# A fp32 encoder block as weight products by Strassen's scheme: activation forms, weight parts and product sums put in another order on VectorE and ScalarE

## The chip, the core and the metric

One core of a Trainium2 chip runs the whole block in one launch. The metric is device microseconds of one execution. In the profile PE is TensorE, PEld its weight loads, DVE is VectorE, ACT is ScalarE, POOL is GpSimd, and SP queues most of the loads.

## The reference

512 tokens of 2048 features pass one encoder block in float32; the feed-forward width is 5632.

```python
h = rms_norm(x, norm_mix); z = h @ w_in                      # q, k, v, u, gates a and b
y_a = chunked_rel_attention(q, k, v, rel_bias)               # 16 heads of 64
y_b = multiscale_pool(u, pool_w, pool_scale)
merged = sigmoid(z_ga) * (y_a @ w_branch_a) + sigmoid(z_gb) * (y_b @ w_branch_b)
x = x + merged @ w_out                                       # 2048 x 2048
gu = rms_norm(x, norm_ffn) @ w_gate_up                       # 2048 x 2*5632
x = x + (silu(gu[:, :5632]) * gu[:, 5632:]) @ w_down         # 5632 x 2048
return rms_norm(x, norm_final)
```

## The kernel before

Each float32 operand is used as two parts, a high one rounded to TensorE's fp32r type and a low one, the rest: ScalarE copies the high part out (`hi`, `hiw`), VectorE subtracts (`lo`, `low`). A product of two such operands is three matmuls.

The first 988 us make the projections of `w_in`, the attention, the pooling and the two branch products, panel by panel. The last gate panels and branch-a panels stand apart (`N_TAIL`): first the gates, then the branch products, whose results make `merged`.

From there on the kernel runs **jobs**. A job multiplies 512 tokens by a block of 1024 weight rows and 2 x 512 weight columns, split two by two in tokens, rows and columns, and needs seven block products instead of eight (`PRODUCTS`: P1, P5, P6, P3, P7, P2, P4, in this order). The left factor of a product is a **form**: a sum or difference of activation blocks (P1 is a11, P5 a22-a21, P6 minus that plus a11, P7 a11-a21, P3, P2, P4 in the same way), split in high and low. The right factor is a weight block or a running sum of blocks: the adds L842 to L848 (`t_to`) work in place on the raw blocks r11, r12, r22, r21. A product has two halves, so a job has 14 **steps** of twelve matmuls each (four for the row pairs and token halves, three for the parts). At step i the code

- queues the raw loads of step i+7 (`load2_to`), the add of step i+3 (`t_to`) and the high part of step i+2 (`hi2_to`, L856);
- issues the twelve matmuls (L893 to L895) into a PSUM bank pair;
- at a product's end takes the bank out: copies of P1, P5, P6 and, without accumulation, of P4 on ScalarE (L899, L904, L909, L929), sums of P3, P7, P2 and else P4 on VectorE (L911, L916, L922, L926);
- calls `step()`, which lets every waiting piece of other work (a generator) issue one portion;
- queues the low part of step i+2 (`lo2_to`, L864).

There are three buffers each for the high and the low parts, two bank pairs of kind x (P1, P6, P7 and P4 of one job share one), one of kind y (P5 with P3, then P2), and two single banks a for transposes. The jobs come in the order of a list: 4 with `w_out` (o), 11 with the first 1024 rows of `w_gate_up` (g 0), then 11 with its other rows (g 1) and among them those with `w_down` (d), two for each block of 1024 hidden rows. 5632 hidden rows are five and a half blocks; the half block (one half a product, seven steps a job) comes last.

The other work: after each o job of the second row block the new x is squared for the norm, transposed on TensorE (L953), scaled (L962) and made into forms for `w_gate_up` (`x1_ready`); after each g 1 job silu and gate times up (`hidden`, L1017, L1020), transposes, and forms for `w_down` (`build_down`). `build_forms` makes a form a step for one half of a form set: the copy L737 of a portion is on ScalarE, the sums L729 to L732 and the subtractions L740, L742 on VectorE; a subtraction waits for the copy of the same form. In the last two jobs POOL multiplies by the weight of the last norm (L1079), and after the last product the row norms and eight output tiles each on ScalarE (L1101) and VectorE (L1098) follow.

Of the kernel before, what the change touches and what calls it, by code (L numbers as in the profile page):

```python
# [40 lines left out]
N_TAIL = 3  # L41
# [5 lines left out]
def hybrid_block_kernel(  # L47
# [672 lines left out]
    def build_forms(forms, h, half):  # L720
# [8 lines left out]
        plan = [("P1", a11, 1, None), ("P5", s, 1, lambda: tt(s, a22, a21, op=ALU.subtract)),  # L729
                ("P6", s, -1, lambda: tt(s, s, a11, op=ALU.add)),  # L730
                ("P3", s, 1, lambda: tt(s, s, a12, op=ALU.subtract)),
                ("P7", s3, 1, lambda: tt(s3, a11, a21, op=ALU.subtract)), ("P2", a12, 1, None), ("P4", a22, 1, None)]  # L732
        for p, src, sign, make in plan:
            if make:
                make()
            hi, lo = forms[p][:, prs, 0], forms[p][:, prs, 1]
            nc.scalar.activation(hi, src, AF.Copy, scale=float(sign))  # L737
            yield
            if sign > 0:
                tt(lo, src, hi.bitcast(F32), op=ALU.subtract)  # L740
            else:
                nc.vector.scalar_tensor_tensor(lo, src, -1.0, hi.bitcast(F32), op0=ALU.mult, op1=ALU.subtract)  # L742
# [125 lines left out]

    def run_job(j):
        forms = j.forms  # L870
        X = Y = Z = None
        a = p5 = u2 = None
        for n, p in enumerate(PRODUCTS):
            if p == "P1":
                X = ps = bank2("x")
            elif p == "P5":
                Y = ps = bank2("y")
            elif p == "P2":
                Z = ps = bank2("y")
            else:  # L880
                ps = Y if p == "P3" else X
            for h in range(j.nh):
# [3 lines left out]
                hi2_to(i + SPLIT)  # L886
                hi, lo = wide(hi_t.pop(-1 - i)), wide(lo_t.pop(-1 - i))
                for t in range(2):
                    for k in range(2):
# [5 lines left out]
                        mm(ps[:, t], fl, hi[:, k], start=False, stop=last, skip_group_check=True)  # L895
                if h == j.nh - 1:
                    if p == "P1":
                        a = ctile()
                        nc.scalar.activation(a, X, AF.Copy)  # L899
                        if j.acc:  # L900
                            nc.gpsimd.dma_start(a, j.acc["11"], accum_op=ALU.add)
                    elif p == "P5":
                        p5 = ctile()
                        nc.scalar.activation(p5, Y, AF.Copy, scale=-1.0)  # L904
                        if j.acc:
                            nc.gpsimd.dma_start(p5, j.acc["22"], accum_op=ALU.add)
# [283 lines left out]
    while active or later:  # L1190
        step()
# [23 lines left out]
```

## Time and profile before

| | |
|---|---|
| median of 3 runs | 2541.85 us (2539.72 to 2542.73) |
| the profiled execution | 2541.46 us, of which the span of its instructions is 2539.5 us |
| busy share of the span, PE / PEld / DVE / ACT / POOL | 97% / 79% / 68% / 46% / 6% |
| mean granted clock of TensorE | 0.992 |
| HBM | 289.44 MB read, 60.86 MB written |

Matmuls overlap, so a busy PE says little of how much it could still gain; the starts of consecutive matmuls say more.

### The profile page before, as it was taken

The page shows a single profiled execution, that of the slowest core. Times are in us where ns is not written, and L with a number is a line of the kernel's source. Part 1 is how long each engine was busy: PE and PEld are TensorE (multiplying, and loading weights), DVE is VectorE, ACT ScalarE, POOL GpSimd, SP SyncE. Part 2 cuts the span into 40 slices and gives each one's busy share as a digit, 9 for nine tenths or more (in the row PEclk, how much of TensorE's full clock was granted, in tenths as well). Part 3 has the DMA queues.
Part 4 walks back from the last instruction along what each step waited for, and adds up shares of the span by engine and source line. Part 5 has one row for each costly group of instructions (what it writes and reads, how often), then busy time and mean ns, then how long its engine had stood idle before and what let it go on. Part 6 is the DMA issues. An engine that isn't in the chain of part 4 may idle for free.

```text
span 2539.5 us, 29049 instructions
## 1 busy us (share of the span) xinstructions
PE 2455.2 (97%) x11221; PEld 2002.9 (79%) x11221; DVE 1732.6 (68%) x1996; ACT 1163.4 (46%) x1499; POOL 151.3 (6%) x242
## 2 busy tenths in 40 slices
PE   9999999999999998999999999999999999999995
PEld 7888888888888887777788888877878778787773
DVE  6445556533343327978877777888897888879885
ACT  5444443322232224466545445555554555555554
POOL 0000000000000000110000000000000001000014
PEclk9999999999999999999999999999999999999997
DMA  5322222323333336664443543645645646637374
GB/s 175 96 86 78 86 92 85 94 92 100 94 101 115 107 106 199 187 211 136 179 163 141 195 156 146 203 117 167 161 145 144 171 133 165 182 104 203 100 214 118
DMA packets 203146, 352.20 MB, mean 139 GB/s; under 512 B 11304, under 2 KB 95856, under 8 KB 202880
## 3 DMA queue, kind: packets, MB, share of 16 engines
q1 hardware_dynamic: 177760, 263.76, 30.9%
q0 software_dynamic: 24096, 84.49, 14.2%
q8 instruction: 88, 1.44, 0.2%
q10 hardware_dynamic: 1152, 2.10, 0.2%
q14 instruction: 50, 0.41, 0.0%
HBM read 289.44 MB, written 60.86 MB: 138 GB/s over the span
## 4 chain that ended last, share of the span: by engine, by line
PE 86%; DVE 8%; issue 3%; ACT 2%; DMA 1%; ACTq 0%; SPq 0%; POOL 0%; DVEq 0%; POOLq 0%
PE psd L211 10%; PE psd L212 10%; PE psd L213 10%; PE psx L893 8%; PE psx L894 8%; PE psx L895 8%; PE psy L893 7%; PE psy L895 7%; PE psy L894 7%; DVE low L864 3%; PE psd L423 1%; DVE fP L740 1%; PE psd L425 1%; PE psd L424 1%; ACT hiw L856 1%
## 5 line engine op out<-in xcount | busy, mean ns | idle before, releaser
L864 DVE TENSOR_TENSOR low<-r,hiw 128x1024 fp32r<-128x1024 f32 x518 | 630.4, 1225 | 133.7 <-ACT hiw L856 131.4
L856 ACT ACTIVATE hiw<-r 128x1024 fp32r<-128x1024 f32 x518 | 546.5, 1057 | 377.0 <-PE psx L895 157.6
L893 PE MATMUL psx<-low,fP 128*128 128x512 f32 x1184 | 471.7, 398 | 29.7 <-DVE low L864 25.2
L894 PE MATMUL psx<-hiw,fP 128*128 128x512 f32 x1184 | 463.3, 391 | 0.0
L895 PE MATMUL psx<-hiw,fP 128*128 128x512 f32 x1184 | 463.1, 391 | 0.0
L168 DVE TENSOR_TENSOR lo<-raw,hi 128x1024 fp32r<-128x1024 f32 (+1 forms) x161 | 195.9, 1218 | 322.8 <-ACT hi L159 322.6
L893 PE MATMUL psy<-low,fP 128*128 128x512 f32 x888 | 353.1, 398 | 23.9 <-DVE low L864 21.8
L159 ACT ACTIVATE hi<-raw 128x1024 fp32r<-128x1024 f32 (+1 forms) x161 | 169.2, 1053 | 427.5 <-PE psd L213 309.7
L895 PE MATMUL psy<-hiw,fP 128*128 128x512 f32 x888 | 348.3, 392 | 0.0
L894 PE MATMUL psy<-hiw,fP 128*128 128x512 f32 x888 | 348.1, 392 | 0.0
L211 PE MATMUL psd<-xh,lo 128*128 128x512 f32 x864 | 341.5, 395 | 0.0
L213 PE MATMUL psd<-xl,hi 128*128 128x512 f32 x864 | 336.7, 390 | 0.0
L212 PE MATMUL psd<-xh,hi 128*128 128x512 f32 x864 | 336.6, 390 | 0.0
L893 PEld LDWEIGHTS psx<-low,fP 128*128 128x128 f32 x1184 | 222.9, 188 | 103.5 <-DVE low L864 55.4
L895 PEld LDWEIGHTS psx<-hiw,fP 128*128 128x128 f32 x1184 | 223.1, 188 | 48.1
L894 PEld LDWEIGHTS psx<-hiw,fP 128*128 128x128 f32 x1184 | 223.1, 188 | 42.3
L893 PEld LDWEIGHTS psy<-low,fP 128*128 128x128 f32 x888 | 168.1, 189 | 68.4 <-DVE low L864 29.0
L895 PEld LDWEIGHTS psy<-hiw,fP 128*128 128x128 f32 x888 | 168.1, 189 | 36.1
L894 PEld LDWEIGHTS psy<-hiw,fP 128*128 128x128 f32 x888 | 168.5, 190 | 32.9
L211 PEld LDWEIGHTS psd<-xh,lo 128*128 128x128 f32 x864 | 162.2, 188 | 36.3 <-issue 2.4
L213 PEld LDWEIGHTS psd<-xl,hi 128*128 128x128 f32 x864 | 162.2, 188 | 34.3
L212 PEld LDWEIGHTS psd<-xh,hi 128*128 128x128 f32 x864 | 162.4, 188 | 31.9
(207 smaller groups left out, 2810.7 us busy)
## 6 DMA issues: line engine op xcount, KB each, us to landing
r<-in_w_gate_up SPq DMA_DIRECT2D x176, 512.0 KB, 7.6
raw<-in_w_in SPq DMA_DIRECT2D x127, 512.0 KB, 3.6
r<-in_w_down SPq DMA_DIRECT2D x88, 512.0 KB, 6.5
x1d<-c POOLq DMA_DIRECT2D x48, 512.0 KB, 8.0
gp<-c POOLq DMA_DIRECT2D x44, 512.0 KB, 6.0
c<-gp POOLq DMA_DIRECT2D x33, 512.0 KB, 5.2
r<-in_w_out SPq DMA_DIRECT2D x32, 512.0 KB, 9.2
raw<-in_w_branch_b SPq DMA_DIRECT2D x16, 512.0 KB, 3.3
```

The source lines that it names most:

```text
L159: nc.scalar.activation(hi_t[i][:, :m], raw_t[i][:, :m], AF.Copy)
L168: nc.vector.tensor_tensor(lo_t[i][:, :m], raw_t[i][:, :m], hi_t[i].bitcast(F32)[:, :m], op=ALU.subtract)
L211: mm(ps, wl, ah, start=start, stop=False)
L212: mm(ps, wh, ah, start=False, stop=False)
L213: mm(ps, wh, al, start=False, stop=stop)
L423: mm(o, XH[kk][:, tok], hi[:, k], start=first, stop=False, skip_group_check=True)
L424: mm(o, XH[kk][:, tok], lo[:, k], start=False, stop=False, skip_group_check=True)
L856: nc.scalar.activation(hi_t[-1 - i], source(i), AF.Copy)
L864: nc.vector.tensor_tensor(lo_t[-1 - i], source(i), hi_t[-1 - i].bitcast(F32), op=ALU.subtract)
L893: mm(ps[:, t], fh, lo[:, k], start=first, stop=False, skip_group_check=True)
L894: mm(ps[:, t], fh, hi[:, k], start=False, stop=False, skip_group_check=True)
L895: mm(ps[:, t], fl, hi[:, k], start=False, stop=last, skip_group_check=True)
```

## The change

- `build_forms`: the order of the forms is now P1, P5, P7, P6, P2, P3, P4. Each step issues ScalarE's copy of one form and VectorE's subtraction of the form of the step ahead. Both differences that need no other form are made first.
- `run_job`: the low part of step i+2 is queued ahead of the matmuls of step i, and the end of a product (`evacuate`) is put on a list that is run in the `step()` of the following step, so it is queued one step later than before and behind that step's add, high and low part.
- `x1_turned`: the transposes of x1 wait until both token halves of a column block are there, and turn 512 tokens at a time with one ScalarE copy per 128 columns; the squares are a piece of work by themselves.
- Order of the jobs: the half block of hidden rows is now the first of `w_down` (it needs the first g 1 job alone), and the d jobs follow the odd g 1 jobs. The forms of the last block go to form set B, when all g jobs have run.
- `N_TAIL` is 4: four gate panels, then four branch-a panels.
- Last norm: the multiplication by its weight is on VectorE; the last block takes it with its scaling in one operation; nine of the sixteen output tiles go through ScalarE, none of them from the last block. The ends of P2 and P4 of the last job are issued without the delay.

```diff
@@ build_forms
+        plan = [("P1", a11, 1), ("P5", s, 1), ("P7", s3, 1), ("P6", s, -1), ("P2", a12, 1), ("P3", s, 1), ("P4", a22, 1)]
+        def low(p, src, sign):
+            hi, lo = forms[p][:, prs, 0].bitcast(F32), forms[p][:, prs, 1]
+            if sign > 0:
+                tt(lo, src, hi, op=ALU.subtract)
+            else:
+                nc.vector.scalar_tensor_tensor(lo, src, -1.0, hi, op0=ALU.mult, op1=ALU.subtract)
+        tt(s, a22, a21, op=ALU.subtract)
+        tt(s3, a11, a21, op=ALU.subtract)
+        for n, (p, src, sign) in enumerate(plan):
+            nc.scalar.activation(forms[p][:, prs, 0], src, AF.Copy, scale=float(sign))
+            if n:
+                low(*plan[n - 1])
+            if n == 2:
+                tt(s, s, a11, op=ALU.add)
+            elif n == 4:
+                tt(s, s, a12, op=ALU.subtract)
+            yield
+        low(*plan[-1])
@@ evacuate, new
+        if p in ("P1", "P5", "P6"):
+            blk = {"P1": "11", "P5": "22", "P6": "12"}[p]
+            o[blk] = ctile()
+            nc.scalar.activation(o[blk], ps, AF.Copy, scale=1.0 if p == "P1" else -1.0)
+            if j.acc and p != "P6":
+                nc.gpsimd.dma_start(o[blk], j.acc[blk], accum_op=add)
+            return
+        blk = {"P3": "12", "P7": "22", "P2": "11", "P4": "21"}[p]
+        if p != "P4":
+            nc.vector.tensor_tensor(o[blk], o[blk], ps, op=add if p == "P2" else sub)
...
+        j.done(blk, o[blk])
@@ run_job
                 hi2_to(i + SPLIT)
+                lo2_to(i + SPLIT)
                 hi, lo = wide(hi_t.pop(-1 - i)), wide(lo_t.pop(-1 - i))
...
+                step()
                 if h == j.nh - 1:
...
-                        nc.vector.tensor_tensor(u2, u2, Y, op=ALU.subtract)
...
-                step()
-                lo2_to(i + SPLIT)
+                    later.append(lambda p=p, ps=ps: evacuate(j, p, ps, o))
+                    if j is jobs[-1] and p in ("P2", "P4"):
+                        step()
@@ x1
+    def x1_turned(p, fb, cs):
+        half = yield from new_half()
+        for n in range(4):
+            ps = bank2("a")
+            for tt in range(NT):
+                nc.tensor.transpose(ps[:, tt * P:(tt + 1) * P], cs[tt // 2][:, tt % 2, n * P:(n + 1) * P], ident)
+            yield
+            m = KD + p * 8 + fb * 4 + n
+            nc.scalar.activation(half[:, n // 2, n % 2], ps, AF.Copy, scale=gains[:, m:m + 1])
@@ build_down, the order of the jobs
-        b, h = p // 2, p % 2
-        while b < n_down - 1 and down_run[0] < 2 * b:
+        b, h = (p + 1) // 2, (p + 1) % 2 if p else 0
+        last = b == n_down - 1
+        while gates_run[0] < NG if last else down_run[0] < 2 * b:
...
-        if p >= 2 and p % 2 == 0 and p < NG - 1:
-            order += [("d", p // 2 - 1, 0), ("d", p // 2 - 1, 1)]
+        if p % 2 and p < NG - 2:
+            order += [("d", p // 2, 0), ("d", p // 2, 1)]
...
-            npair = min(NPAIR, (KF - 8 * b) // 2)
+            npair = NPAIR if b else NPAIR // 2
@@ last_done
-                nc.gpsimd.tensor_tensor(y[:, t], y[:, t], gf[:, f0:f0 + 512], op=ALU.mult)
-                yield
+                if (p, blk) != FINAL:
+                    nc.vector.tensor_tensor(y[:, t], y[:, t], gf[:, f0:f0 + 512], op=ALU.mult)
+                    yield
```

**A g 1 job in which forms are built.** On VectorE, in the second g 1 job, around the end of P3 (the sum of c and psy, L911 before, L889 now); low232 to low235 are the low parts of P7's and P2's four steps, fP1 to fP7 forms, s their sums. Before:

```order
L864 TENSOR_TENSOR low232_12352<-r12_916_12080,hiw232_12335 128x1024
L911 TENSOR_TENSOR c_933_12319<-c_933_12319,psy_926_12229 128x1024
L740 TENSOR_TENSOR fP5_934_12323<-s_935_12329,fP5_934_12323 128x2x256
L730 TENSOR_TENSOR s_935_12329<-s_935_12329,half_924_12220 128x512
L864 TENSOR_TENSOR low233_12375<-r12_919_12103,hiw233_12356 128x1024
L742 SCALAR_TENSOR_TENSOR fP6_934_12324<-s_935_12329,fP6_934_12324 128x2x256
L731 TENSOR_TENSOR s_935_12329<-s_935_12329,half_924_12220 128x512
L864 TENSOR_TENSOR low234_12396<-r21_928_12253,hiw234_12379 128x1024
```

And of the changed kernel:

```order
L872 TENSOR_TENSOR low233_12341<-r12_918_12084,hiw233_12339 128x1024
L735 TENSOR_TENSOR fP1_934_12325<-half_925_12224,fP1_934_12325 128x2x256
L872 TENSOR_TENSOR low234_12361<-r21_927_12231,hiw234_12359 128x1024
L889 TENSOR_TENSOR c_933_12322<-c_933_12322,psy_923_12203 128x1024
L735 TENSOR_TENSOR fP5_934_12326<-s_935_12332,fP5_934_12326 128x2x256
L746 TENSOR_TENSOR s_935_12332<-s_935_12332,half_925_12224 128x512
L856 TENSOR_TENSOR r21_927_12231<-r21_927_12231,r11_914_12026 128x1024
L872 TENSOR_TENSOR low235_12385<-r21_929_12255,hiw235_12383 128x1024
L735 TENSOR_TENSOR fP7_934_12329<-s3_935_12333,fP7_934_12329 128x2x256
```

The low part of P7's second half (low233) stood behind the sum of P3, a form and a form's sum; now it, and the next one too (low234), stand ahead of that sum.

**The first job.** On VectorE, from the last branch-a panel (L664, L665: the gated result `merged`) into the first `w_out` job; low1 and low2 are the low parts of its steps P1 (second half) and P5 (first half), r11 its running sums. Before:

```order
L665 TENSOR_TENSOR sg_633_7318<-sg_571_5718,sg_633_7318 128x512
L864 TENSOR_TENSOR low1_7576<-r11_643_7498,hiw1_7574 128x1024
L742 SCALAR_TENSOR_TENSOR fP6_634_7330<-s_646_7533,fP6_634_7330 128x2x256
L731 TENSOR_TENSOR s_646_7533<-s_646_7533,half_638_7372 128x512
L740 TENSOR_TENSOR fP3_634_7331<-s_646_7533,fP3_634_7331 128x2x256
L732 TENSOR_TENSOR s3_646_7534<-half_638_7372 128x512
L740 TENSOR_TENSOR fP7_634_7332<-s3_646_7534,fP7_634_7332 128x2x256
L740 TENSOR_TENSOR fP2_634_7333<-half_638_7372,fP2_634_7333 128x2x256
L740 TENSOR_TENSOR fP4_634_7334<-half_638_7372,fP4_634_7334 128x2x256
L842 TENSOR_TENSOR r11_642_7496<-r11_642_7496,r12_647_7605 128x1024
L842 TENSOR_TENSOR r11_643_7498<-r11_643_7498,r12_648_7607 128x1024
L864 TENSOR_TENSOR low2_7642<-r11_642_7496,hiw2_7616 128x1024
```

And of the changed kernel:

```order
L735 TENSOR_TENSOR fP3_632_7261<-s_642_7463,fP3_632_7261 128x2x256
L664 TENSOR_TENSOR sg_631_7248<-psd_646_7518,sg_631_7248 128x512
L665 TENSOR_TENSOR sg_631_7248<-sg_571_5718,sg_631_7248 128x512
L872 TENSOR_TENSOR low1_7586<-r11_644_7511,hiw1_7584 128x1024
L735 TENSOR_TENSOR fP4_632_7264<-half_636_7302,fP4_632_7264 128x2x256
L850 TENSOR_TENSOR r11_643_7509<-r11_643_7509,r12_647_7605 128x1024
L850 TENSOR_TENSOR r11_644_7511<-r11_644_7511,r12_648_7607 128x1024
L872 TENSOR_TENSOR low2_7618<-r11_643_7509,hiw2_7616 128x1024
L852 TENSOR_TENSOR r11_643_7509<-r11_643_7509,r22_649_7609 128x1024
```

Five form subtractions and two form sums stood between low1 and the adds of the job's P5; one subtraction is left there, since a branch-a panel more runs while the forms are made.

**The last job.** On POOL before, the multiplications by the last norm's weight gf behind the accumulating loads:

```order
L906 DMA c_1306_18322<-x1d122_5896 128x1024
L913 DMA c_1307_18341<-x1d112_5894 128x1024
L1079 TENSOR_TENSOR c_1306_18322<-c_1306_18322,gf_18124 128x512 x2
L1079 TENSOR_TENSOR c_1304_18297<-c_1304_18297,gf_18124 128x512
L1079 TENSOR_TENSOR c_1307_18341<-c_1307_18341,gf_18124 128x512
L1079 TENSOR_TENSOR c_1304_18297<-c_1304_18297,gf_18124 128x512
L1079 TENSOR_TENSOR c_1308_18377<-c_1308_18377,gf_18124 128x512
L1079 TENSOR_TENSOR c_1307_18341<-c_1307_18341,gf_18124 128x512
L1079 TENSOR_TENSOR c_1308_18377<-c_1308_18377,gf_18124 128x512
```

On VectorE in the changed kernel, at the last job's P7 and P2 (L889), with low516 and low517 the last weight parts:

```order
L872 TENSOR_TENSOR low516_18333<-r21_1304_18203,hiw516_18331 128x1024
L889 TENSOR_TENSOR c_1306_18239<-c_1306_18239,psx_1301_18142 128x1024
L1085 TENSOR_TENSOR c_1306_18239<-c_1306_18239,gf_17860 128x512
L872 TENSOR_TENSOR low517_18354<-r21_1305_18221,hiw517_18352 128x1024
L1085 TENSOR_TENSOR c_1307_18276<-c_1307_18276,gf_17860 128x512
L1085 TENSOR_TENSOR c_1306_18239<-c_1306_18239,gf_17860 128x512
L889 TENSOR_TENSOR c_1303_18200<-c_1303_18200,psy_1308_18329 128x1024
L1085 TENSOR_TENSOR c_1307_18276<-c_1307_18276,gf_17860 128x512
L1085 TENSOR_TENSOR c_1303_18200<-c_1303_18200,gf_17860 128x512 x2
```

The multiplications now stand between VectorE's sums and weight parts; POOL keeps only its loads.

## Rows read from the trace of the kernel before

**Rows 1.** The page, busy time by engine and the granted clock in 40 slices.
```profile
PE 2455.2 (97%) x11221; PEld 2002.9 (79%) x11221; DVE 1732.6 (68%) x1996; ACT 1163.4 (46%) x1499; POOL 151.3 (6%) x242
...
PEclk9999999999999999999999999999999999999997
```

**Rows 2.** Windows: us, busy us (count) of PE, PEld, DVE, ACT, POOL; clock, DMA, GB/s.
```profile
987.80:1079.81 92.01, 81.97 (x337) 63.91 (x336) 80.57 (x84) 46.37 (x54) 11.75 (x14) 0.96 0.71 205
...
1117.98:1257.18 139.20, 128.63 (x570) 100.78 (x568) 119.59 (x129) 88.25 (x138) 9.10 (x15) 0.99 0.47 161
1333.38:1371.48 38.10, 38.10 (x170) 31.32 (x168) 29.63 (x26) 18.52 (x18) 2.13 (x4) 1.00 0.45 166
1638.18:1807.47 169.29, 161.60 (x721) 129.55 (x720) 143.41 (x138) 90.68 (x105) 11.00 (x13) 1.00 0.50 139
1807.47:1970.67 163.20, 158.56 (x705) 128.08 (x704) 139.00 (x133) 88.28 (x100) 11.97 (x14) 1.00 0.56 155
...
2297.07:2463.97 166.90, 159.71 (x706) 128.05 (x704) 145.14 (x143) 91.83 (x107) 11.95 (x14) 1.00 0.57 160
2463.97:2517.76 53.79, 44.57 (x169) 34.20 (x167) 36.28 (x27) 26.24 (x42) 22.13 (x19) 0.90 0.54 111
2517.76:2539.52 21.76, 0.16 (x1) 0.00 (x0) 8.39 (x23) 10.86 (x21) 7.04 (x6) 0.59 0.50 193
```

**Rows 3.** Timeline of PE at four transposes between two steps.
```profile
1644.88 0.60 PE L953 MATMUL psa<-ident,c 128*128 128x128 f32 x4
1645.23 0.48 PE L893 MATMUL psy<-low,fP 128*128 128x512 f32 x1
1645.55 0.39 PE L894 MATMUL psy<-hiw,fP 128*128 128x512 f32 x1
```

**Rows 4.** Timeline, DVE and PE at a stall: start, us, what [idle before <-releaser].
```profile
1663.13 0.39 PE L893 MATMUL psx<-low,fP 128*128 128x512 f32 x1
1663.33 1.22 DVE L911 TENSOR_TENSOR c<-c,psy 128x1024 f32<-128x1024 f32 x1 [0.94 <-PE psy L895]
1664.47 0.69 DVE L740 TENSOR_TENSOR fP<-s,fP 128x512 fp32r<-128x512 f32 x1
1665.19 0.69 DVE L730 TENSOR_TENSOR s<-s,half 128x512 f32<-128x512 f32 x1
1665.80 1.22 DVE L864 TENSOR_TENSOR low<-r,hiw 128x1024 fp32r<-128x1024 f32 x1
1667.07 0.50 PE L893 MATMUL psx<-low,fP 128*128 128x512 f32 x1 [1.06 <-DVE low L864]
```

**Rows 5.** Timeline of DVE, ACT and PE at the first weight-product job.
```profile
996.73 2.35 DVE L842 TENSOR_TENSOR r<-r,r 128x1024 f32<-128x1024 f32 x2
998.06 2.19 ACT L856 ACTIVATE hiw<-r 128x1024 fp32r<-128x1024 f32 x2 [2.14 <-DVE r L842]
999.15 1.23 DVE L864 TENSOR_TENSOR low<-r,hiw 128x1024 fp32r<-128x1024 f32 x1
1000.43 0.79 PE L893 MATMUL psy<-low,fP 128*128 128x512 f32 x1 [6.46 <-DVE low L864]
```

**Rows 6.** Timeline of POOL, DVE and ACT in the last 40 us.
```profile
2500.47 2.83 POOL L1079 TENSOR_TENSOR c<-c,gf 128x512 f32<-128x512 f32 x2
2501.85 2.55 DVE L864 TENSOR_TENSOR low<-r,hiw 128x1024 fp32r<-128x1024 f32 x1 [1.77 <-ACT hiw L856]
...
2520.93 1.28 ACT L348 ACT_TABLE_LOAD   x1
...
2527.59 0.20 ACT L348 ACTIVATE fin<-r 128x2 f32<-128x2 f32 x1 [0.42 <-ACT c L1101]
...
2528.49 0.16 DVE L252 SCALAR_TENSOR_TENSOR fin<-r,fin 128x2 f32<-128x2 f32 x1
...
2529.96 0.72 ACT L1101 ACTIVATE c<-c,fin 128x512 f32<-128x512 f32 x1 [0.42 <-DVE c L1098]
...
2533.38 0.72 ACT L1101 ACTIVATE c<-c,fin 128x512 f32<-128x512 f32 x1 [0.41 <-ACT c L1101]
```

More of the change, by code (lines that the diff above doesn't have):

```diff
@@ L867, in hybrid_block_kernel, with evacuate @@
     TOK = (slice(0, P), slice(P, 2 * P))
+    def evacuate(j, p, ps, o):
+        add, sub = ALU.add, ALU.subtract
+        if p in ("P1", "P5", "P6"):
[8 more added lines that the diff above has]
+            nc.vector.tensor_tensor(o[blk], o[blk], ps, op=add if p == "P2" else sub)
+        elif not j.acc:
+            o[blk] = ctile()
+            nc.scalar.activation(o[blk], ps, AF.Copy)
+        elif j is jobs[-1]:
+            for t in range(2):
+                nc.vector.tensor_tensor(o[blk][:, t], o[blk][:, t], ps[:, t], op=add)
+        else:
+            nc.vector.tensor_tensor(o[blk], o[blk], ps, op=add)
+        if j.acc and p == "P3":
+            nc.gpsimd.dma_start(o[blk], j.acc[blk], accum_op=add)
+        if j.acc and p == "P7":
+            o["21"] = ctile()
+            nc.sync.dma_start(o["21"], j.acc["21"])
+        j.done(blk, o[blk])
     def run_job(j):
-        forms = j.forms
-        X = Y = Z = None
-        a = p5 = u2 = None
+        forms, o = j.forms, {}
+        X, Y = bank2("x"), None
         for n, p in enumerate(PRODUCTS):
[L874 to L881, printed above, removed]
+            if p in ("P5", "P2"):
+                Y = bank2("y")
+            ps = Y if p in ("P5", "P3", "P2") else X
             for h in range(j.nh):
@@ L944, in hybrid_block_kernel, with turned @@
     fin = const.tile([P, 2, NT], F32, name="fin")
-    halves = {}
-    def turned(src, th, half, scale):
+    def turned(src, th, half):
         for c2 in range(2):
@@ L971, in x1_ready @@
             yield
[L972 to L982 removed]
+    def x1_turned(p, fb, cs):
[4 more added lines that the diff above has]
+                nc.tensor.transpose(ps[:, tt * P:(tt + 1) * P], cs[tt // 2][:, tt % 2, n * P:(n + 1) * P], ident)
+            yield
+            m = KD + p * 8 + fb * 4 + n
+            nc.scalar.activation(half[:, n // 2, n % 2], ps, AF.Copy, scale=gains[:, m:m + 1])
+        if p not in gu_forms:
+            gu_forms[p] = new_forms("AB"[p])
+        yield from build(gu_forms[p], fb, half)
     def wait_then(n, g):
@@ L1025, in hidden @@
             hid[p] = yield from new_half()
-        yield from turned(up, th, hid[p], None)
+        yield from turned(up, th, hid[p])
         if th == 1:
@@ L1068, in hybrid_block_kernel @@
     ys = {}
+    FINAL = (1, "21")
     def last_done(p, blk, c):
@@ L1072, in last_done @@
         ys[p, blk] = y = c
+        f0 = p * 1024 + fb * 512
         def rest():
@@ L1189, in hybrid_block_kernel @@
         down_run[0] += what == "d"
+        gates_run[0] += (what, b) == ("g", 1)
     while active or later:
```

87 lines of the change are left out of this document (16 added, 71 removed).

## The prediction

> **What bounds the kernel now.** I read the page first: TensorE is busy 97% of the span at a granted clock of almost 1 throughout, VectorE 68% [rows 1]. That share hides what is lost, so I then read windows cut at the starts of jobs [rows 2]. An undisturbed job (1333.38 to 1371.48, eight more like it) takes 38.10 us for its 168 matmuls, 2.72 us a step; VectorE is busy 29.63 us of it. Four transposes cost 0.35 us, and the matmul after them starts its successor 0.32 instead of 0.23 us later [rows 3], so 0.44; a half turned in 16 transposes costs 1.76. What the other windows take beyond 38.10 a job and these transposes is stall:
>
> - A, the first two o jobs (987.80 to 1079.81): 92.0 - 76.2 = 15.8.
> - B, the second o job of the second row block and two g 0 jobs (1117.98 to 1257.18): 139.2 - 114.3 - 4 x 1.76 = 17.9.
> - C, from the second g 1 job to the half-size jobs (1638.18 to 2463.97, 20 jobs, 11 turned halves): 825.8 - 762.0 - 19.4 = 44.4. One period of two g and two d jobs is the row of 163.20; two more are like it.
> - D, the two half-size jobs at the end: 53.8 - 38.1 = 15.7.
> - E, what follows the last product: 21.8 us.
>
> So about 94 us of stall can be had, and part of 22. The timeline at a stall of C [rows 4] shows its kind: PE starts a step at 1663.13, and the low part of the next step stands fourth in VectorE's queue: behind the sum of P3, which can only start when PE has ended the product (1663.33), a form's subtraction and a form's sum. It starts at 1665.80, and PE waits for it until 1667.07, 1.06 us idle. VectorE runs without a hole there, one 1024-wide operation every 1.14 us, a half-width one every 0.61, or 0.72 if it needs the one before. At the first job [rows 5] the same queue holds the adds of P5 until 996.73, and PE is idle 6.46 us; the granted clock of that window is 0.96 [rows 2], so some matmuls after it ran at the lower level.
>
> The Trainium skill, Perfetto Trace Analysis, section Optimization Strategy, holds that a bubble that repeats on the engine that should be saturated can mean that there are too few buffers for the next tile. By that the stalls of C would stay whole, since the change adds no buffer. The row above speaks for the queue's order, not the buffers; it is the third case below.
>
> **The change, part by part.** *Low part ahead, sum a step later.* The high part of step i+2 needs the buffer of step i-1, so it starts with step i, and is there 0.2 + 1.1 us later (two took 2.19 [rows 5]); the low part then takes 1.23 and PE sees it 0.1 to 0.2 later: 2.6 of the 5.44 us until it is needed. VectorE may thus lag 2.8 us. Where a sum must leave a bank before the next product may start in it (P3's sum before P2, P7's before P4), the sum stands behind that low part: 1.14 less, 1.7. Before, the low part came after the sum, which left 2.72 - 0.2 - 1.14 - 1.4 = 0: every form operation at a product's end was a stall, which is what the timeline at the stall shows [rows 4].
>
> I count VectorE's work step by step in a g 1 job with forms. From P2's first low part on, the changed order gives between low parts 4.62, 2.88, 3.48, 1.74, 4.02, 3.53 (forms and sums together), then in the next job, with gate times up, 4.07, 2.93, 1.79 us, against 2.72. The lag grows to 1.9, 2.1, 2.8, 1.8, 3.1, 4.0, 5.3, 5.5 and falls after. PE must wait for what exceeds 2.8: 2.7 us. Dependent half-width operations (some eight at 0.1) make it 3.3, restarts (the first matmul after the stall took 0.1 longer, at four stalls) 3.7. The other g job of a period stays under the limit: its largest lag is about 1. That happens five times, 18.5; after the last g job the forms of both halves of the last block are made in the d jobs, 3.7 again by the same count. C falls from 44.4 to 22. The bounds: nothing left but the restarts, 2, and no gain, 44.4; I stay with the count, since it uses durations of the trace [rows 4] and a limit that follows from three buffers.
>
> *Forms pipelined.* The subtraction no longer waits for its copy. It saves VectorE's holes, not work: 7 subtractions and 4 sums of 0.61 are 6.7 us a half, as now. I cost it at nothing beyond the count above, which has no holes. If it didn't work, a hole of 0.7 us at up to seven forms would come back in each of 19 builds, up to 90 us; the copy has a whole step as cover.
>
> *B.* Four halves are made into forms without a break over about 29 steps. VectorE's common work is 26 x 1.14 / 14 = 2.11 a step: 61.3 + 4 x 6.7 + 1.5 for dependence = 89.6; PE needs 29 x 2.72 + 3 x 1.76 = 84.2 and can be 2.8 ahead: 2.6 us is the lower bound, 17.9 the upper. ScalarE has squares, copies and forms here as well (88.25 us in the window of 139.20, in bursts), so I take 6.5. x1 turned at once starts the forms of a column block later, but the first one is due only at the first g job, three steps (8 us) after it is made; each us beyond that would be a stall once. The transposes stay 64, and ScalarE's copies become fewer and wider, both off the path.
>
> *A.* A fourth branch-a panel stands behind the last gate panel, so two sets of forms are nearly done when the first job starts; the panels' sum is unchanged. Then VectorE has, from the end of the last panel: 0.2, two half-width operations 1.3, low1 1.14, one form 0.61, an add 1.14, then 1.25 for the high and 1.23 for the low part: 6.9, and PE needs it at 5.44. With the small stall of low1 and restarts that leaves 2. The forms of the second row block in the first 16 steps: 16 x 2.11 + 13.4 + 1.5 - 16 x 2.72 - 2.8 = 2.4, taken as 3. A falls from 15.8 to 5; bounds 1 and 15.8.
>
> *D.* The half-size jobs become ordinary ones at the end, where the last norm's products put 8 x 0.61 us a job on VectorE (about 34 of 38 us): 1 us. The half block now runs early, without accumulation. Each product is one step there, so a sum has 2.72 us to leave its bank, behind an add and a low part. For P3: the low part ends 2.5 after the step's start, the add of P4 at 3.65, which is 0.9 into the next step; high part 2.0, low part 3.3, sum 4.6: 1.95 late. P7's sum comes out 0.8 late in the same way, P5's copy on ScalarE 0.6. Two jobs: 7 us. D falls from 15.7 to 8; bounds 1 and 15.7. That POOL's multiplications go from beside VectorE is in this: a low part beside them took 2.55 us instead of 1.22 [rows 4, 6].
>
> *E.* From the end of P2 of the last job, P4's two steps run 5.45 us. Under them: P2's sum (to 1.35), two squares on ScalarE at some 0.75 (to 2.9), the table load 1.28 and the root with its refinement, 1.06 from 2527.59 to the end of 2528.49 [rows 6]: 5.4, nothing left over. ScalarE then puts out three tiles, 1.14 apart (2529.96 to 2533.38 are three), squares P4's block (to 10.4), the second root, six tiles; the last starts at 16.8. Before, 6.14 us passed from the last tile's start (2533.38) to the span's end (2539.52 [rows 2]). 16.8 + 6.14 - 5.45 = 17.5 instead of 21.8: 4.1 less, with 0.2 for slips. If the cover under P4 were gone, the first root's 3 us come back.
>
> Sum: A 10.8, B 11.4, C 22.4, D 7.7, E 4.1: 56.4. The profiled execution took 2541.5, which lies 0.4 under the median of the runs: **2485 us**.
>
> **The rivals.** *The order takes all of it.* If VectorE's count is too high (holes of the dependent operations vanish, PE's transposes give it time), A 2, B 3, C 6, half jobs 3.5 are left: another 26, so 2459. For it: busy 38 to 39 us a g job is just under PE's 39.9. Against it: the lag peaks within a job, not on average.
>
> *The bubbles stay* (too few buffers, or VectorE full in B and C whatever the order). Then the gain is D, E and the first job's part of A (6.46 idle, and up to 3.7 for the clock, if 0.08 of 92 us ran at half speed, less the 2 left: taken as 7.5): 19.3, so 2522. For it: VectorE is busy 119.59 of 139.20 in B and 139.00 of 163.20 in a period of C, and each low part still waits for one of three buffers. Against it: the timeline of the stall, where the wait is the queue [rows 4].
>
> *Slower: the sums come too late.* A sum is queued a step later and behind an add and a low part; with P2 and P4 PE then waits for the bank of P3 or P7, which it never did for long. 38 jobs (half ones counted singly) have two such places, 76. Without forms the sum ends 3.7 us into 5.44, so 1.7 are spare; if ScalarE's high part came 2.7 us late everywhere (its queue has the copies ahead), it were 76 x 1.0 = 76 lost against 56: 2561. The point is 0.74 us a place. Against it: ScalarE is busy 18.52 of 38.10 us in an undisturbed job.
>
> *It changes nothing:* what is saved in front is waited for in the next stage. I see no stage that runs at a fixed time; the loads are seven steps ahead and stay so.
>
> **How the numbers follow.** Forecast 0.55, all of it 0.15, bubbles stay 0.18, slower 0.07, nothing 0.05. The forecast's own range is 2470 to 2502 (a third of each of B and C either way). The 80% range, 2460 to 2522, reaches to the second and third case; outside lie half of each, and the last two. A change under 0.2% (5 us) could not be told from none here. Faster 0.89, same 0.04, slower 0.07.
>
> **What would show it.** Right: a g 1 job with forms at 40 to 44 us instead of 45; low parts that VectorE starts before the sum of the product that has ended; no idle PE of over 3 us near the first job; half-size jobs of 20 to 24 us after the second g 1 job; 17 to 18 us behind the last product. Wrong: PE idle behind sums (L889) or ScalarE's copies in ordinary jobs; periods in C still of 163; a lower granted clock in new places.

## Result and the profile after

The changed kernel takes 2500.76 us (median of 4 runs, 2500.62 to 2501.57) against 2541.15; the ratio is 0.9842 [0.9825, 0.9859]. The forecast was 2485 with a range of 2460 to 2522: right in its sign and inside its range, with 40 us of gain where 56 were expected. The profiled execution took 2500.83 us, its span 2499.0.

The page of the changed kernel, which answers to [rows 1]: hardly anything is to be seen in it.

```profile
PE 2438.6 (98%) x11221; PEld 2007.9 (80%) x11221; DVE 1724.8 (69%) x2010; ACT 1158.7 (46%) x1484; POOL 129.8 (5%) x226
...
PEclk9999999999999999999999999999999999999998
```

Windows cut at the starts of jobs, as in [rows 2] (columns as there): the first two o jobs, the second row block of o with two g 0 jobs, an undisturbed job, the second g 1 job, the two half-size jobs, a period of two g 1 and two d jobs, the last job, the tail.

```profile
987.60:1069.42 81.82, 77.83 (x337) 62.52 (x336) 76.11 (x78) 42.62 (x48) 11.82 (x14) 1.00 0.75 223
1069.42:1235.13 165.71, 161.52 (x737) 131.93 (x736) 147.61 (x155) 106.04 (x147) 13.88 (x22) 1.00 0.57 189
1349.38:1387.45 38.07, 38.07 (x169) 31.53 (x168) 29.54 (x26) 18.53 (x18) 2.15 (x4) 1.00 0.48 170
1615.93:1657.58 41.65, 40.56 (x185) 33.05 (x184) 37.52 (x39) 23.70 (x30) 2.58 (x3) 1.00 0.63 181
1657.58:1710.84 53.26, 44.01 (x186) 34.47 (x185) 39.30 (x36) 26.56 (x30) 5.21 (x6) 0.94 0.54 136
1710.84:1871.71 160.87, 157.59 (x705) 129.07 (x704) 138.37 (x134) 87.83 (x100) 13.01 (x15) 1.00 0.54 148
2436.83:2480.06 43.23, 40.42 (x169) 32.28 (x167) 35.08 (x35) 22.76 (x36) 2.59 (x3) 0.96 0.32 76
2480.06:2499.03 18.97, 0.16 (x1) 0.00 (x0) 7.28 (x25) 9.57 (x17) 0.00 (x0) 0.60 0.58 222
```

The same account as in the prediction (a window, less 1.76 us a turned half and, in the changed kernel, 38.08 a job instead of 38.10) gives the stalls below, in us. B is here the four jobs from 1069.42, C the nineteen g 1 and d jobs of full size from the second g 1 job on, without the last job; the half-size jobs stood at the end before. The last column is the first experiment, below.

| | before | forecast | after | silu later |
|---|---|---|---|---|
| A, two o jobs | 15.8 | 5 | 5.7 | 5.7 |
| B | 17.9 | 6.5 | 6.4 | 6.4 |
| C | 44.4 | 22 | 26.5 | 16.3 |
| half-size jobs | 15.7 | 7 | 13.4 | 9.1 |
| last full job | in C | 1 | 5.1 | 0.8 |
| E, tail | 21.8 | 17.5 | 19.0 | 17.2 |
| sum | 115.6 | 59 | 76.1 | 55.5 |

A and B came out as forecast. What is missing sits in C (4.5), the half-size jobs (6.4), the last job (4.1) and the tail (1.5). Of the signs that were named, a g 1 job with forms at 40 to 44 us is there (41.65) and the idle time of over 3 us near the first job is gone, but the first half-size job takes 32.0 us instead of 20 to 24, and the tail 19.0 instead of 17 to 18. Two of the signs against it are there too: PE waits for sums (L889) twelve times, 9.1 us in all and nine of them in jobs of full size, and the granted clock is lower in new places, the half-size jobs behind the second g 1 job (0.94) and the last job (0.96).

The timeline of VectorE and PE around the end of P7 in the second g 1 job shows the new order at work, and answers to [rows 4]:

```profile
1649.60 1.22 DVE L872 TENSOR_TENSOR low<-r,hiw 128x1024 fp32r<-128x1024 f32 x1
...
1650.74 1.21 DVE L889 TENSOR_TENSOR c<-c,psx 128x1024 f32<-128x1024 f32 x1
...
1651.87 0.69 DVE L737 SCALAR_TENSOR_TENSOR fP<-s,fP 128x512 fp32r<-128x512 f32 x1
...
1652.01 0.50 PE L924 MATMUL psx<-low,fP 128*128 128x512 f32 x1 [0.32 <-DVE c L889]
```

The low part now runs ahead of the sum and the form, and PE waits for the bank here, 0.32 us; before, it idled for low parts that stood behind sums, 1.06 us at the end of P3 [rows 4]. The job takes 41.65 us instead of 45.03.

But here is ScalarE in the first half-size job (DVE, ACT and PE, from 1664.59):

```profile
1664.59 1.23 DVE L872 TENSOR_TENSOR low<-r,hiw 128x1024 fp32r<-128x1024 f32 x1
...
1665.73 1.21 DVE L897 TENSOR_TENSOR c<-c,psx 128x1024 f32<-128x1024 f32 x1
...
1666.98 1.33 ACT L1016 ACTIVATE c<-c,r 128x512 f32<-128x512 f32 x2 [2.42 <-DVE c L897]
1668.22 1.04 ACT L864 ACTIVATE hiw<-r 128x1024 fp32r<-128x1024 f32 x1
1669.17 1.00 ACT L883 ACTIVATE c<-psx 128x1024 f32<-128x1024 f32 x1
1669.29 1.23 DVE L872 TENSOR_TENSOR low<-r,hiw 128x1024 fp32r<-128x1024 f32 x1 [1.68 <-ACT hiw L864]
...
1670.22 0.80 PE L924 MATMUL psx<-low,fP 128*128 128x512 f32 x1 [5.02 <-ACT c L883]
...
1670.81 0.63 PE L925 MATMUL psx<-hiw,fP 128*128 128x512 f32 x1
...
1671.24 0.63 PE L926 MATMUL psx<-hiw,fP 128*128 128x512 f32 x1
```

The sum of the last g 1 product (L897) stands behind a low part and ends at 1666.94. Silu (L1016) reads it, and was queued on ScalarE at once; ScalarE waits 2.42 us for it. Behind silu stand the next high part and the copy that empties P1's bank, so VectorE waits 1.68 for the high part and PE 5.02 for the bank. The matmuls after it then start 0.43 us apart instead of 0.23: the granted clock of the window of both half-size jobs is 0.94.

The last job has the same pattern with the last norm's square (L1083) in silu's place:

```profile
2443.05 1.22 DVE L897 TENSOR_TENSOR c<-c,psx 128x1024 f32<-128x1024 f32 x1
...
2444.63 0.63 ACT L1083 ACTIVATE sq<-c 128x512 f32<-128x512 f32 x1 [4.36 <-DVE c L897]
...
2445.26 1.04 ACT L864 ACTIVATE hiw<-r 128x1024 fp32r<-128x1024 f32 x1
...
2445.39 0.69 DVE L1085 TENSOR_TENSOR c<-c,gf 128x512 f32<-128x512 f32 x1 [1.13 <-ACT sq L1083]
...
2448.41 0.50 PE L924 MATMUL psy<-low,fP 128*128 128x512 f32 x1 [2.21 <-DVE low L872]
```

Here VectorE waits for ScalarE as well: the multiplication by the norm's weight may not overwrite the block before its square is taken.

### The profile page after: what moved, and what is told of

Read it like the earlier page. It is cut to its first block, busy times and chain, and to the rows that moved or that the text cites. A ratio compares the mean times of both kernels' runs of the same rounds, so it can differ in the third digit from the quotient of the medians.

```text
span 2499.0 us, 28903 instructions
## 1 busy us (share of the span) xinstructions
PE 2438.6 (98%) x11221; PEld 2007.9 (80%) x11221; DVE 1724.8 (69%) x2010; ACT 1158.7 (46%) x1484; POOL 129.8 (5%) x226
## 4 chain that ended last, share of the span: by engine, by line
PE 83%; DVE 11%; issue 3%; ACT 2%; DMA 1%; SPq 0%; ACTq 0%; DVEq 0%
PE psd L211 10%; PE psd L213 10%; PE psd L212 10%; PE psx L924 8%; PE psx L925 8%; PE psx L926 8%; PE psy L924 6%; PE psy L925 6%; PE psy L926 6%; DVE low L872 4%; PE psd L423 1%; PE psd L425 1%; PE psd L424 1%; DVE c L889 1%; ACT hiw L864 1%
```

## The experiments

The kernel before, run beside them, had medians of 2540.94, 2541.83 and 2540.68 us in the three groups (the first four, the next four, the last three).

**1. Silu and squares a step later.** The rival to the ScalarE theory is the forecast's own explanation of what is left, VectorE's count.

```diff
     def hidden(p, th, gate, up):
+        yield
         for t in range(2):
...
-            active.append(wait_then(3 if blk == "12" else 0, rest()))
+            active.append(wait_then(3 if blk == "12" else 1, rest()))
```

> The changed kernel, in which silu (two operations per token half of a g 1 job) and the squares of the last norm are issued one step later, so that the next step's high part stands ahead of them on ScalarE. ScalarE theory: what is left of the stalls in the d jobs that follow a g 1 job, in the half-size jobs and in the last job comes from ScalarE, where such an operation waits for a sum that VectorE now makes a step later, with a high part queued behind it. Then the first half-size job falls from 32.0 to 22 to 25 us, the last job from 43.0 to about 39, a d job after an odd g 1 job from 43.08 to 41 or less, and the time from 2501 to about 2480. VectorE theory (the forecast's count: too much form work at the end of a g 1 job, and in the half-size jobs single-step products whose sums leave the bank late): VectorE's work is the same, so all of these stay within 1 us of what they are, and the time stays at 2497 to 2503.

Measured 2480.93 us, 0.9763 [0.9749, 0.9778] of before. The windows of the half-size jobs, of a period, of the last job and of the tail:

```profile
1657.04:1705.98 48.94, 41.95 (x186) 32.77 (x184) 39.74 (x37) 26.93 (x31) 5.21 (x6) 1.00 0.57 143
1705.98:1864.88 158.90, 156.99 (x706) 128.97 (x705) 137.90 (x134) 88.86 (x100) 13.01 (x15) 1.00 0.55 150
2422.82:2461.69 38.87, 38.57 (x169) 31.19 (x167) 34.72 (x38) 23.18 (x35) 2.59 (x3) 1.00 0.35 84
2461.69:2478.93 17.24, 0.16 (x1) 0.00 (x0) 6.18 (x21) 8.04 (x14) 0.00 (x0) 0.57 0.63 243
```

VectorE has the same work, and 20 us are gone: the ScalarE theory holds for the last job (38.87 us) and for the tail, which starts with its row norm in time. The first half-size job falls to 27.6 only, the d job after an odd g 1 job to 42.2, so something else is left there. The added `yield` moves all that follows silu by a step as well (products, transposes, forms), so ScalarE's order is not the only thing that changes; but the wait itself goes. Silu waited 72.4 us in all for the two sums that it reads, and 6.3 here.

**2. The queue order undone.**

```diff
-                lo2_to(i + SPLIT)
...
+                if h == j.nh - 1:
+                    evacuate(j, p, ps, o)
                 step()
-                if h == j.nh - 1:
-                    later.append(lambda p=p, ps=ps: evacuate(j, p, ps, o))
...
+                lo2_to(i + SPLIT)
```

> The changed kernel with only the queue order undone: a low part is queued behind the step's other work again, and a bank is taken out at once at the end of its product. The forecast's way (the queue order carries the gain in B and C): the g 1 jobs with forms go back to about 45 us and the time rises by 20 to 35, to 2520 to 2535, less what the half-size jobs get back (some 8 us by the ScalarE theory, since sums come at once again). Rival (the other parts carry the gain: forms in a new order, x1 turned 512 tokens at a time, the order of the jobs): the time stays within 8 us of 2501.

Measured 2527.44 us. A period takes 166.1 us, an odd g 1 job 46.1 to 46.3, and A and B 2.7 and 4.1 us more; the half-size jobs fall to 45.9. Silu still waits for its sum in the first of them, 3.69 us, but PE idles 2.46 us for the low part behind it, where it idled 5.02 for the bank. The queue order is worth 26.7 us net. It has two halves, the low part ahead and the bank taken out a step later, and no run here undoes one of them alone.

**3. The order of the forms undone.** build_forms as before; everything else stays changed.

```diff
-            if n:
-                low(*plan[n - 1])
-            if n == 2:
-                tt(s, s, a11, op=ALU.add)
...
+            if make:
+                make()
+            nc.scalar.activation(hi, src, AF.Copy, scale=float(sign))
+            yield
...
```

> The changed kernel with only the order of the forms undone (a form's copy, sum and subtraction in the old sequence). The forecast's way: it was costed at nothing, because a form's copy has a whole step as cover in either sequence, and VectorE's work is the same 6.7 us a half: the time stays at 2498 to 2505. Rival (it carries a part of the gain: a hole of 0.7 us on VectorE at some forms of 19 builds comes back): over 2507, up to 2590 if every form had one.

Measured 2584.64 us, slower than before (1.0171 [1.0156, 1.0186]). The rival holds, and the time is near its price for a hole at every form; the holes, however, are others. The timeline of VectorE, ScalarE and PE in the second g 1 job (L730 the sum of a form, L738 its copy, L857 a high part, L865 a low part):

```profile
1678.38 0.69 DVE L730 TENSOR_TENSOR s<-half 128x512 f32<-128x512 f32 x1
...
1679.10 0.63 ACT L738 ACTIVATE fP<-s 128x512 fp32r<-128x512 f32 x1 [2.50 <-DVE s L730]
...
1679.64 1.04 ACT L857 ACTIVATE hiw<-r 128x1024 fp32r<-128x1024 f32 x1
...
1680.71 1.23 DVE L865 TENSOR_TENSOR low<-r,hiw 128x1024 fp32r<-128x1024 f32 x1 [1.65 <-ACT hiw L857]
...
1686.04 1.23 DVE L865 TENSOR_TENSOR low<-r,hiw 128x1024 fp32r<-128x1024 f32 x1 [0.51 <-ACT hiw L857]
...
1687.32 0.50 PE L917 MATMUL psy<-low,fP 128*128 128x512 f32 x1 [0.94 <-DVE low L865]
```

The copy waits on ScalarE for the sum that VectorE has just made, the high part stands behind the copy, and VectorE's next operation is the low part that needs it: 1.65 us without work, in a stretch where VectorE has none to spare. From the first job on, ScalarE's copies wait 189 us for the sums of forms, and 48 in the changed kernel. No subtraction waits for its copy; VectorE waits for the weights' high part, at four or five places in a build, 4.3 us or more together, where the changed kernel has two or none in most builds.

**4. The old order of the jobs**, with the half block last, in the changed kernel.

```diff
-        if p % 2 and p < NG - 2:
-            order += [("d", p // 2, 0), ("d", p // 2, 1)]
+        if p >= 2 and p % 2 == 0 and p < NG - 1:
+            order += [("d", p // 2 - 1, 0), ("d", p // 2 - 1, 1)]
...
-            npair = NPAIR if b else NPAIR // 2
+            npair = min(NPAIR, (KF - 8 * b) // 2)
```

> The changed kernel with the old order of the jobs: the half block last, d jobs behind the even g 1 jobs. The forecast's way: the half-size jobs at the end are worth 15.7 us of stall against 8, so the time rises by about 7, to 2508. ScalarE theory: the half-size jobs lose 13 us in the new place and the last job 5, as much as before at the end; in the old place they have no silu ahead of them, but the last norm's squares, so the time stays within 5 us of 2501.

Measured 2499.69 us: 1.1 less, by a median of 4 runs each. In this kernel the new order of the jobs is worth nothing.

**5. Queue order and forms both undone** (the diffs of 2 and 3 together).

> The changed kernel with the queue order and the order of the forms both undone; x1, the order of the jobs, the gate panels and the last norm stay changed. Theory (the two belong together: a form's copy on ScalarE waits for its sum on VectorE, with the next high part queued behind the copy; the old place of the low part, behind the sum, lies over that round trip, the new place ahead of the sum leaves it open, and the new order of the forms closes it again): with the old place the order of the forms is worth little, and the time is that of the run with the queue order alone undone, 2527, within 7 us. Rival (the order of the forms saves its 84 us by itself): 2590 or more.

Measured 2519.96 us. That is at the lower end of the theory's range (2527 less 7), and the rival is far off. With experiments 2 and 3 this makes a square:

| us | forms old | forms new |
|---|---|---|
| low part behind (old) | 2519.96 | 2527.44 |
| low part ahead (new) | 2584.64 | 2500.76 |

Alone, each of the two edits makes this kernel slower, by 7.5 and 64.7; together they gain 19.2. The other 21 of the 40 us are those of the remaining parts: A falls from 15.8 to 7.5 without the pair, B from 17.9 to 11.1, the tail from 21.8 to 17.6, and the half-size jobs from 15.7 to 6.9, against some 7 more in C and the last job.

**6. Three gate panels instead of four.**

```diff
-N_TAIL = 4
+N_TAIL = 3
```

> The changed kernel with three gate and branch-a panels at the end instead of four. The forecast's way (with the fourth panel two form sets are nearly done when the first job starts): the first job goes back from 41.3 us to 45 to 49, and the time rises by 4 to 9, to 2505 to 2510. Rival (the order of forms and queue alone took the stall from the first job): the first job stays at 41 to 43, and the time within 2.5 us of 2501.

Measured 2506.78 us; the first job takes 46.67 us instead of 41.32, and A is 11.0 instead of 5.7. The fourth panel does what the forecast's account of A says, and is worth half of the 10.1 that A gained.

**7. No sums in the form builds**, on top of experiment 1. A form is made from one block alone, so the kernel leaves out a part of the scheme and doesn't compute the block.

```diff
-        tt(s, a22, a21, op=ALU.subtract)
-        tt(s3, a11, a21, op=ALU.subtract)
+        s, s3 = a22, a11
...
-            if n == 2:
-                tt(s, s, a11, op=ALU.add)
-            elif n == 4:
-                tt(s, s, a12, op=ALU.subtract)
```

> The kernel with silu and squares a step later, and beside that without the four sums and differences of activation blocks in each of the 19 form builds (a form is then made from one block alone): 4 operations of 0.61 to 0.69 us less on VectorE a build, everything else as it was. VectorE theory (what is left of the stalls in A, B and in the g 1 and d jobs with forms, some 3.7 us a period of four jobs, is VectorE's work over PE's time there): each of these stalls falls by most of 2.4 us, the period from 158.9 to about 156.5, and the time from 2481 to 2458 to 2467. Rival (what is left is a wait for one of three buffers or for ScalarE): the time stays within 5 us of 2481.

Measured 2463.69 us, 17.2 less. The window of a period:

```profile
1698.05:1855.49 157.44, 156.49 (x706) 129.18 (x704) 132.72 (x125) 88.52 (x100) 13.01 (x15) 1.00 0.56 151
```

A falls from 5.7 to 2.6, B from 6.4 to 1.8, C from 16.3 to 6.8, with the buffers as they were: most of what is left there after experiment 1 is VectorE's work. The sums' readers on ScalarE wait less here too, but the trace of experiment 1 speaks for VectorE: ahead of the largest stall of its period (1.65 us, at 1794.80) VectorE runs without a hole for 19 us. The half-size jobs fall by 1 us only, to 48.0, so their rest is something else. The Trainium skill's sentence on bubbles (Perfetto Trace Analysis, section Optimization Strategy), that a repeating one can mean too few buffers, does not hold for these: the buffers were not touched, and the bubbles of A, B and C fell from 28.4 to 11.2 us with VectorE's work.

**8. ScalarE's copies at once.** On top of experiment 1.

```diff
+                if h == j.nh - 1 and p in ("P1", "P5", "P6"):
+                    evacuate(j, p, ps, o)
                 step()
-                if h == j.nh - 1:
+                if h == j.nh - 1 and p not in ("P1", "P5", "P6"):
```

> The kernel with silu and squares a step later, and ScalarE's copies of P1, P5 and P6 issued at once at the end of their product, ahead of the next high part; VectorE's sums stay a step later. Theory (in the half-size jobs PE waits 3.2 us for a copy that stands behind a high part, which waits for VectorE's add): the two half-size jobs fall from 48.9 to 44 to 46 us, the time to 2476 to 2479. Rival (a copy ahead delays each high part by its 1.0 us, and where VectorE has no spare that comes out): the jobs with forms get longer by 0.5 to 1 us each, and the time is 2482 to 2488.

Measured 2486.41 us, which is in the rival's range, but neither was right: the half-size jobs get longer, 54.1 us, while C stays at 16.3 and A and B grow by 0.6 and 1.0. The timeline in the first half-size job:

```profile
1676.34 1.21 DVE L889 TENSOR_TENSOR c<-c,psy 128x1024 f32<-128x1024 f32 x1
...
1677.61 0.50 PE L924 MATMUL psy<-low,fP 128*128 128x512 f32 x1 [3.13 <-DVE c L889]
```

The wait for ScalarE's copy is now one for VectorE's sum of P3, and the matmuls after it again start 0.43 us apart. My theory of the half-size jobs fell: the copy was only what came last. That they got longer is mostly the clock: twenty of their matmuls start 0.43 us apart, none in experiment 1, which makes 4 of the 5.2 us (the granted clock of the two jobs is 0.94 and 0.87). PE's idle time rose from 7.0 to 8.3 us.

**9. x1 as before**, in the changed kernel: a token half is turned as soon as it is there.

```diff
-    def x1_turned(p, fb, cs):
+    def x1_ready(p, b, c):
...
-            active.append(wait_then(3 if b == "12" else 1, x1_squares(p, b, c)))
-            if b[0] == "2":
-                fb = int(b[1]) - 1
-                active.append(wait_then(2, x1_turned(p, fb, (ready["1" + b[1]], c))))
+            active.append(wait_then(4 if b == "12" else 2, x1_ready(p, b, c)))
```

> The changed kernel with only x1's part undone (the transposes of a token half as soon as it is there, with two ScalarE copies each, squares and turning one piece of work). The forecast's way (costed at nothing: the transposes stay 64, ScalarE's copies are off the path): B stays at its 7.6 us of stall within 1.5, and the time at 2499 to 2503. Rival (with queue order and forms both undone B had 12.4 us of stall left of the 19.3 of before, so x1's part is worth some 7 there): B goes to 12 to 16, and the time to 2505 to 2510.

Measured 2505.65 us; B is 10.4 instead of 6.4 (11.7 instead of 7.6 as the expectation counts, with four transposes at 0.36 us), just under the rival's 12, and the time is the rival's. Of PE's waits between 1060 and 1250 us the largest is for a ScalarE copy of turned x1, ahead of a transpose:

```profile
PE psa L954 <- ACT half L963: 3.1, 1, 3.1
```

**10. The form sums on GpSimd.** On top of experiment 1.

```diff
-        tt(s, a22, a21, op=ALU.subtract)
+        nc.gpsimd.tensor_tensor(s, a22, a21, op=ALU.subtract)
...
```

> The kernel with silu and squares a step later, and the four sums and differences of each form build on GpSimd instead of VectorE. VectorE theory with engines that don't disturb each other: as without these sums, the stalls fall by up to 17 us, 2464 to 2470 (a sum takes GpSimd about 1.4 us, which a step covers). Rival (contention: before, a low part beside GpSimd's multiplications took 2.55 us instead of 1.22, so each sum takes VectorE 1.3 us where its own operation takes 0.65): VectorE loses some 2.6 us more in each build, and the time is 2485 to 2500.

Measured 2506.06 us, 25 more, beyond the rival's range. The timeline of GpSimd, VectorE, ScalarE and PE in a g 1 job:

```profile
1788.38 2.13 POOL L746 TENSOR_TENSOR s<-s,half 128x512 f32<-128x512 f32 x1 [2.39 <-DVE fP L735]
...
1789.29 2.31 DVE L872 TENSOR_TENSOR low<-r,hiw 128x1024 fp32r<-128x1024 f32 x1
...
1790.54 0.63 ACT L742 ACTIVATE fP<-s 128x512 fp32r<-128x512 f32 x1 [2.87 <-POOL s L746]
1791.08 1.04 ACT L864 ACTIVATE hiw<-r 128x1024 fp32r<-128x1024 f32 x1
...
1792.78 0.50 PE L924 MATMUL psx<-low,fP 128*128 128x512 f32 x1 [0.97 <-DVE c L889]
```

Both things happen: the low part takes 2.31 us instead of 1.22, 1.1 us more for an operation that cost VectorE 0.69 itself; and ScalarE waits 2.87 us for the slower sum, again with a high part behind it. The Trainium skill (Perfetto Trace Analysis, section Optimizing Scalar/DVE Operations) warns that GpSimd and VectorE share a read port, so that moving work between the two may not help; the trace agrees, with the 2.31 us; that the port is the cause no run here shows.

**11. The last norm's multiplications on GpSimd.** On top of experiment 1.

```diff
-                    nc.vector.tensor_tensor(y[:, t], y[:, t], gf[:, f0:f0 + 512], op=ALU.mult)
+                    nc.gpsimd.tensor_tensor(y[:, t], y[:, t], gf[:, f0:f0 + 512], op=ALU.mult)
```

> The kernel with silu and squares a step later, and the last norm's fourteen multiplications by its weight back on GpSimd. The forecast's way (a low part beside them takes up to 2.55 us instead of 1.22): the last jobs lose 1.5 to 5 us, the tail stays, and the time is 2482 to 2486. Rival (GpSimd's work is hidden, and VectorE has fourteen operations of 0.61 less): the time stays at 2478 to 2481.5.

Measured 2487.09 us, 6.2 more than experiment 1 and 1.1 over the forecast's range (the profiled spans differ by 7.3): 3.4 in the last job, as the forecast's way has it, 1.5 in the tail, which was to stay, and 2.5 in the half-size jobs, where nothing was changed (below, on the clock).

## Why the prediction was right, and where not

- *What bounds the kernel* was right: the stalls, not PE's share. In A, B and C a place in VectorE's queue set most of them; experiment 7 takes work out of that queue, and 28.4 us of stall become 11.2.
- *A* (5 forecast, 5.7): right in size, but the panel alone does half of it: A is 11.0 without the panel (experiment 6) and 8.4 without the queue order (experiment 2).
- *Low part ahead* (C from 44.4 to 22): the count on VectorE was a little high. With ScalarE's wait out of the way C is 16.3, a period 3.1 us over its matmuls and transposes where 3.7 were counted (by its own terms the count gives 3.9: 2.7, eight times 0.1, and 0.4). But in the changed kernel itself C is 26.5, because of a term that the count doesn't have.
- **The step that failed**: the cost of "sum a step later". I followed the late sum to the bank that it empties, and not to ScalarE's operations that read it. Silu and the squares follow the sum in the same portion of work, the high part behind them starts only after them (1668.22 and 2445.26 in the rows above), and that is what VectorE and PE wait for. Experiment 1 prices this at 19.8 us; by the account it is 10.2 in C, 4.3 in the half-size jobs, 4.3 in the last job and 1.7 in the tail. Of the 4.3 in the half-size jobs 2.0, and of those in the last job 1.4, are matmuls 0.43 us apart after the wait; experiment 11, with the same place of silu, has 2.2 us of such matmuls in the half-size jobs, so that these 2 us need not be silu's. The wait was not new. Rows of the kernel before (us in all, times, longest) show silu (L1017) waiting for the sums of P4 and P2 of each g 1 job:

```profile
ACT c L1017 <- DVE c L926: 33.4, 11, 3.3
ACT c L1017 <- DVE c L922: 16.7, 11, 1.9
```

  The later sums made this 48.4 and 24.0 us. No run moves silu in the old queue order, so how much of the 19.8 us the later sums brought, and how much was there before, stays open. Against the rival "sums come too late" I had set ScalarE's busy time, 18.52 of 38.10 us; a busy share says nothing about an operation that stands and waits at the head of a queue. That rival named the engine rightly; it was wrong in making it all or nothing.
- *Forms pipelined* (nothing): right only as a part of the sum. Left out, it costs 84 us, near the bound of 90, but not by the bound's holes: no subtraction waits for its copy, and VectorE waits for the high part behind the copy instead (1.65 and 0.51 us in the rows of experiment 3), at four or five places in a build. The cover that I named, a whole step for the form's copy, covers the copy, not the high part queued behind it. The trace of before has this pair on ScalarE, near the stall of [rows 4]:

```profile
1665.91 0.63 ACT L737 ACTIVATE fP<-s 128x512 fp32r<-128x512 f32 x1 [3.05 <-DVE s L730]
1666.45 1.04 ACT L856 ACTIVATE hiw<-r 128x1024 fp32r<-128x1024 f32 x1
```

  So the two edits are one edit: the old place of the low part hid the round trip, the new place needs the new order of the forms.
- *B* (6.5, measured 6.4): right in size, wrong in its parts. Without the queue order B is 4.1 more, and without x1's part, costed at nothing, 4.0 more: the transposes' copies were not off the path, PE waited 3.1 us for one.
- *D*: the half block was forecast to lose 7 us in its new place; it loses 13.4, and the last job 5.1 instead of 1, so that the order of the jobs gains nothing (experiment 4). 8.6 of these 18.5 go with ScalarE's wait (experiment 1). About the other 9 us of the half-size jobs: P5's copy and P3's sum each come late when the other does not, as experiment 8 shows, and less form work helps by 1 us only. With the old queue order, in which both are issued at once, 6.1 us are left (experiment 2). Which edit would mend it in the new order stays open.
- *E* (17.5, measured 19.0): the chain was right, but "P2's sum (to 1.35)" was not. P4's steps start at 2474.62, and the rows of the changed kernel show what stood ahead of the sum:

```profile
2474.02 0.69 DVE L1085 TENSOR_TENSOR c<-c,gf 128x512 f32<-128x512 f32 x1 [0.79 <-ACT sq L1083]
...
2476.11 1.29 DVE L1085 TENSOR_TENSOR c<-c,gf 128x512 f32<-128x512 f32 x2
...
2477.32 1.22 DVE L889 TENSOR_TENSOR c<-c,psy 128x1024 f32<-128x1024 f32 x1
...
2482.33 0.16 DVE L252 SCALAR_TENSOR_TENSOR fin<-r,fin 128x2 f32<-128x2 f32 x1
```

  The sum ends at 2478.54, 3.9 us after P4's start, behind three multiplications by the norm's weight, the first of which waited 0.79 us for ScalarE's late square; the first root is there 2.4 us after the last product. In experiment 1 the tail is 17.24 us.

That the forecast of 2485 lies some 4 us from experiment 1 is partly luck: C was counted too high, the half-size jobs too low. And that the changed kernel's time lies in the range says nothing for two terms: forms and x1, both put at nothing, cost 84 and 5 us when they are left out.

## What to carry to other kernels

When a result is made later, follow every reader of it on every engine, and what is queued behind each reader: an operation that is issued at once and waits holds up its whole queue, however idle its engine looks. Two edits that each shift one side of a round trip between two engines are to be priced together; here each alone costs time and both gain. Work that an engine has no room for should be moved only to an engine that doesn't slow the first one.

## What was not expected of the hardware

The clock's answer to a stall is not the same from run to run of nearly the same program. In the kernels of experiments 1 and 11 PE idles 3.19 us at the same place of the first half-size job, behind the same work. The windows of the 5.3 us after it, of experiment 1:

```profile
1670.25:1675.55 5.30, 5.25 (x25) 4.35 (x26) 4.72 (x6) 3.41 (x4) 0.00 (x0) 1.00 0.14 27
```

and of experiment 11:

```profile
1670.10:1675.40 5.30, 5.26 (x12) 4.02 (x13) 4.08 (x5) 1.85 (x2) 0.00 (x0) 0.50 0.14 30
```

The granted clock is 1.00 (2.4 GHz) in the one and 0.50 (1.2 GHz) in the other, 25 matmuls against 12. A stall of some 3 us thus costs itself or 2.5 us more, and a difference of that size between two kernels need not come from the edit. In experiment 8 it makes most of the difference in the half-size jobs.

The other is the price of GpSimd beside VectorE: 128x512 sums took it 1.3 to 3.4 us (VectorE 0.69), and a low part beside one 2.31 instead of 1.22.
